# Binary cross-entropy on one core: compute pieces pipelined across chunk borders with the negation two pieces behind, and the first predictions loaded from SyncE

## The chip, the cores and the metric

The kernel runs on one core of one Trainium2 chip. The metric is device time in microseconds (us); lower is better. Executions of one kernel agree within 0.2% here. DVE is VectorE, ACT is ScalarE, POOL is GpSimd, SP is SyncE; HBM is the chip's main memory, and a DMA queue is the list of transfers that one engine has issued.

## The reference

```python
# pred, target: float32, 8192 x 8192; pred in [0.01, 0.99], target is 0 or 1
pred = np.clip(pred, 1e-7, 1 - 1e-7)
return -(target * np.log(pred) + (1 - target) * np.log(1 - pred))
```

As target is 0 or 1, this is -ln(|target - 1 + pred|), which the kernel computes.

## The kernel before

The 67.1 million elements are 524,288 columns of 128 partitions, cut into chunks of 4096, 4096, 8192, then 30 of 16384, then 8192, 4096, 2048, 1024, 1024. Two rings of 32768 columns hold predictions (float32, overwritten with the result) and targets (cast to bf16 by the load). A ring holds two big chunks, so chunk k+2 can be loaded only after chunk k was stored.

```python
RING = 32768
SUB = 2048
...
    def load(k):
        c, w = at(k), widths[k]            # at(k) = start column % RING
        nc.gpsimd.dma_start(out=ring_t[:, c : c + w], in_=dram(target_f, cols[k], w))
        nc.gpsimd.dma_start(out=ring_p[:, c : c + w], in_=dram(pred_f, cols[k], w))

    def store(k):
        c, w = at(k), widths[k]
        nc.gpsimd.dma_start(out=dram(out_f, cols[k], w), in_=ring_p[:, c : c + w])

    def front(c, w):
        ...                                # DVE: clip; DVE: p = (t - 1) + p; ACT: Abs; ACT: Ln
    def back(c, w):
        ...                                # DVE: p = p * -1

    def compute(k):
        c, w = at(k), widths[k]
        n = max(1, w // SUB)
        s = w // n
        for i in range(n):
            front(c + i * s, s)
            if i:
                back(c + (i - 1) * s, s)
        back(c + (n - 1) * s, s)           # all negations of chunk k before chunk k+1

    with tc.manual_schedule():             # every engine runs its instructions in program order
        stored = loaded = 0
        for k in range(len(widths)):
            ...                            # store what must go, load what then fits
            compute(k)
        ...                                # store the rest
```

Below, t(k), p(k) and "store k" are the target load, prediction load and store of chunk k.

Of the kernel before, what the change touches and what calls it, by code (L numbers as in the profile page):

```python
# [1 line left out]

# [4 lines left out]

EPS = 1e-7



RING = 32768

SUB = 2048


def chunk_widths(total):
    head = [4096, 4096, 8192]
    tail = [8192, 4096, 2048, 1024, 1024]
    big = 16384  # L20
    n = (total - sum(head) - sum(tail)) // big
    widths = head + [big] * n + tail
    assert sum(widths) == total
    return widths


@with_exitstack
def kernel(
    ctx: ExitStack,
    tc: tile.TileContext,  # L30
    pred: bass.AP,
    target: bass.AP,
    out: bass.AP,
):






    nc = tc.nc
    fp32 = mybir.dt.float32
    bf16 = mybir.dt.bfloat16
    Alu = mybir.AluOpType
    Act = mybir.ActivationFunctionType
    P = nc.NUM_PARTITIONS

    R, C = pred.shape
    pred_f = pred.rearrange("r c -> (r c)")
    target_f = target.rearrange("r c -> (r c)")  # L50
    out_f = out.rearrange("r c -> (r c)")
    total = R * C // P

    def dram(flat, col, w):
        return flat[col * P : (col + w) * P].rearrange("(p w) -> p w", p=P)

    pool = ctx.enter_context(tc.tile_pool(name="rings", bufs=1))
    ring_p = pool.tile([P, RING], fp32, name="ring_p", tag="ring_p")
    ring_t = pool.tile([P, RING], bf16, name="ring_t", tag="ring_t")
    warm = pool.tile([1, 8], fp32, name="warm", tag="warm")  # L60
    nc.vector.memset(warm, 1.0)  # L61
    nc.scalar.activation(out=warm, in_=warm, func=Act.Ln)  # L62

    widths = chunk_widths(total)
    cols = [sum(widths[:k]) for k in range(len(widths))]

    def at(k):
        c = cols[k] % RING
        assert c + widths[k] <= RING
        return c  # L70

    def load(k):
        c, w = at(k), widths[k]
        nc.gpsimd.dma_start(out=ring_t[:, c : c + w], in_=dram(target_f, cols[k], w))  # L74
        nc.gpsimd.dma_start(out=ring_p[:, c : c + w], in_=dram(pred_f, cols[k], w))  # L75

    def store(k):
        c, w = at(k), widths[k]
        nc.gpsimd.dma_start(out=dram(out_f, cols[k], w), in_=ring_p[:, c : c + w])  # L79

    def front(c, w):
        p, t = ring_p[:, c : c + w], ring_t[:, c : c + w]
        nc.vector.tensor_scalar(  # L83
            out=p, in0=p, scalar1=EPS, scalar2=1 - EPS, op0=Alu.max, op1=Alu.min
        )
        nc.vector.scalar_tensor_tensor(  # L86
            out=p, in0=t, scalar=1.0, in1=p, op0=Alu.subtract, op1=Alu.add
        )
        nc.scalar.activation(out=p, in_=p, func=Act.Abs)  # L89
        nc.scalar.activation(out=p, in_=p, func=Act.Ln)  # L90

    def back(c, w):
        p = ring_p[:, c : c + w]
        nc.vector.tensor_scalar(  # L94
            out=p, in0=p, scalar1=-1.0, scalar2=None, op0=Alu.mult
        )

    def compute(k):
        c, w = at(k), widths[k]
        n = max(1, w // SUB)  # L100
        s = w // n
        for i in range(n):
            front(c + i * s, s)
            if i:
                back(c + (i - 1) * s, s)
        back(c + (n - 1) * s, s)



    with tc.manual_schedule():  # L110
        stored = loaded = 0
        for k in range(len(widths)):
            while loaded < len(widths):
                end = cols[loaded] + widths[loaded]
                while stored < k and end > cols[stored] + RING:
                    store(stored)
                    stored += 1
                if end > cols[stored] + RING:
                    break
                load(loaded)  # L120
                loaded += 1
            compute(k)
        while stored < len(widths):
            store(stored)
            stored += 1


# [1 line left out]
_INS = ['pred', 'target']  # L129
_OUTS = [((8192, 8192), 'float32')]  # L130


# [23 lines left out]
```

## Time and profile before

| | before |
|---|---|
| device time | 1870.75 us median (1870.64 to 1871.0, 3 runs) |
| DVE busy, ACT busy | 1178.6 us (63%), 976.3 us (52%) |
| software DMA queue, share of 16 engines | 99.9% |
| HBM traffic | 805.3 MB, 431 GB/s over the span |
| cycle of one big chunk | 58.1 us, of which store, target and prediction about 19.4 us each |

The page of the kernel before: the span; the busy tenths of the DMA engines in 40 slices; the DMA queue; the HBM traffic.

```profile
span 1868.8 us, 1563 instructions
...
DMA  9999999999999999999999999999999999999998
...
q0 software_dynamic: 16416, 671.10, 99.9%
...
HBM read 536.87 MB, written 268.44 MB: 431 GB/s over the span
```

The DMA engines are the bound. In the trace a packet of 65,536 bytes takes 2.418 us, so 16 engines carry 16 x 65,536 / 2.418 us = 433.7 GB/s. The Trainium skill ("DMA: Bandwidth & Descriptors", section "Where 436 GB/s comes from") puts the ceiling of the 16 ports at 435.2 GB/s, with which these packets agree; that it lets HBM bind such transfers at about 358 GB/s does not hold here, where one core moved 431 GB/s, and the measurement decides. (A packet of a target load takes 2.43 us too: it reads 65,536 bytes of float32 but writes only 32,768 of bf16, so here the cast saved no time on the DMA engines.) The engines are busy from the first packet, 2.64 us after the span's start, to the last, 1.45 us before its end.

Why do they never run dry? The timeline of the kernel before around the end of one chunk (start, duration, engine, line, operation; in brackets the idle time before it and what ended it):

```profile
530.47 1.23 DVE L94 TENSOR_SCALAR ring_p<-ring_p 128x2048 f32<-128x2048 f32 x1 [2.78 <-ACT ring_p L90]
532.00 0.54 POOL L79 DMA_DIRECT2D out_dram<-ring_p  x1 [20.43 <-DVE ring_p L94]
532.52 0.55 POOL L74 DMA_DIRECT2D ring_t<-in_target_dram  x1
549.52 1.23 DVE L83 TENSOR_SCALAR ring_p<-ring_p 128x2048 f32<-128x2048 f32 x1 [17.82 <-DMA ring_p<-in_pred_dram]
```

The last negation of a chunk (L94) ends at 531.7. POOL issues its store at 532.00 and the target load two chunks on at 532.52. The next prediction load lands only at 549.5, when DVE starts its clip (L83). So at the landing 17.5 us have passed since more work was queued, and DVE's idle time there costs nothing.

The waits of the kernel before (engine and line, what it waited for: us in total, times, longest):

```profile
POOL ring_p L75 <- DMA out_dram<-ring_p: 1084.9, 30, 37.1
...
POOL out_dram L79 <- DVE ring_p L94: 689.9, 36, 25.7
DVE ring_p L83 <- DMA ring_p<-in_pred_dram: 552.9, 32, 18.8
DVE ring_p L94 <- ACT ring_p L90: 120.8, 73, 3.9
```

DVE's 120.8 us of waits for ACT are what the change is after: mainly at the end of each chunk, DVE waits for ACT with nothing else to do.

### The profile page before, as it was taken

The numbers are of one execution on the slowest core, as the hardware profiler recorded it, in microseconds if no ns is written. First come the engines' busy times: TensorE is split into PE (matmuls) and PEld (weight loads), VectorE is DVE, ScalarE is ACT, GpSimd is POOL, SyncE is SP. The second block draws the span as 40 slices with busy tenths as digits, with TensorE's granted clock in tenths as the row PEclk, the third lists the DMA queues.
The fourth block names the chain that finished last, engine by engine and source line by source line (L and its number), as shares of the span: only waits on it lengthen the run. The fifth ranks groups of instructions, "written<-read, shape, count | busy, mean of one in ns | idle before, by whom it ended". The sixth has DMA issues, their size and how long they took to land.

```text
span 1868.8 us, 1563 instructions
## 1 busy us (share of the span) xinstructions
DVE 1178.6 (63%) x772; ACT 976.3 (52%) x516; POOL 65.4 (3%) x118
## 2 busy tenths in 40 slices
DVE  4557755577555775557755577555776556755595
ACT  3446544565444654446544466444664446644474
POOL 1000000000000000000000000000000000000010
DMA  9999999999999999999999999999999999999998
GB/s 292 359 358 338 348 400 371 337 355 342 393 386 339 341 352 387 384 351 339 345 386 389 351 344 337 383 395 344 352 344 365 400 358 339 354 355 395 374 335 349
DMA packets 16427, 671.19 MB, mean 359 GB/s; under 512 B 1824, under 2 KB 1824, under 8 KB 2720
## 3 DMA queue, kind: packets, MB, share of 16 engines
q0 software_dynamic: 16416, 671.10, 99.9%
q14 instruction: 11, 0.09, 0.0%
HBM read 536.87 MB, written 268.44 MB: 431 GB/s over the span
## 4 chain that ended last, share of the span: by engine, by line
DMA 34%; issue 30%; DVE 27%; ACT 7%; POOL 1%; another core or an unknown queue 1%; POOLq 0%; PEldq 0%
DMA ring_p<-in_pred_dram 32%; DVE ring_p L86 13%; DVE ring_p L94 7%; DVE ring_p L83 7%; ACT ring_p L89 3%; ACT ring_p L90 3%; DMA out_dram<-ring_p 2%; POOL out_dram L79 1%; POOL ring_t L74 1%; POOL ring_p L75 0%; POOLq L151 0%; POOLq L79 0%; PEldq L151 0%
## 5 line engine op out<-in xcount | busy, mean ns | idle before, releaser
L89 ACT ACTIVATE ring_p<-ring_p 128x2048 f32<-128x2048 f32 (+1 forms) x257 | 488.9, 1902 | 876.0 <-DVE ring_p L86 876.0
L83 DVE TENSOR_SCALAR ring_p<-ring_p 128x2048 f32<-128x2048 f32 (+1 forms) x257 | 312.9, 1218 | 552.9 <-DMA ring_p<-in_pred_dram 552.9
L86 DVE SCALAR_TENSOR_TENSOR ring_p<-ring_t,ring_p 128x2048 f32<-128x2048 bf16 (+1 forms) x257 | 586.9, 2284 | 8.8
L90 ACT ACTIVATE ring_p<-ring_p 128x2048 f32<-128x2048 f32 (+1 forms) x257 | 489.2, 1903 | 8.1
L94 DVE TENSOR_SCALAR ring_p<-ring_p 128x2048 f32<-128x2048 f32 (+1 forms) x257 | 313.1, 1218 | 120.8 <-ACT ring_p L90 120.8
L75 POOL DMA_DIRECT2D ring_p<-in_pred_dram x38 | 21.9, 576 | 1094.1 <-DMA out_dram<-ring_p 1084.9
L79 POOL DMA_DIRECT2D out_dram<-ring_p x38 | 22.1, 581 | 700.3 <-DVE ring_p L94 689.9
L74 POOL DMA_DIRECT2D ring_t<-in_target_dram x38 | 21.8, 574 | 5.3 <-DMA ring_t<-in_target_dram 4.4
L62 ACT ACT_TABLE_LOAD x1 | 1.3, 1283 | 0.7 <-PEq L140 0.7
L61 DVE MEMSET warm<- 1x8 f32 x1 | 0.1, 65 | 0.8 <-PEq L140 0.8
L62 ACT ACTIVATE warm<-warm 1x8 f32<-1x8 f32 x1 | 0.2, 207 | 0.0
L140 POOL MEMSET const-float32-0.0<- 128x1 f32 x1 | 0.1, 98 | 0.2 <-issue 0.2
L140 POOL MEMSET const-bfloat16-1.0<- 128x1 bf16 x1 | 0.1, 101 | 0.0
L140 POOL MEMSET const-float32-1.0<- 128x1 f32 x1 | 0.1, 98 | 0.0
L140 POOL MEMSET const-uint8-127<- 128x1 uint8 x1 | 0.1, 98 | 0.0
## 6 DMA issues: line engine op xcount, KB each, us to landing
ring_t<-in_target_dram POOLq DMA_DIRECT2D x30, 4096.0 KB, 55.6
ring_p<-in_pred_dram POOLq DMA_DIRECT2D x2, 4096.0 KB, 29.1
out_dram<-ring_p POOLq DMA_DIRECT2D x2, 4096.0 KB, 30.7
ring_p<-in_pred_dram POOLq DMA_DIRECT2D x3, 2048.0 KB, 20.9
out_dram<-ring_p POOLq DMA_DIRECT2D x3, 2048.0 KB, 53.1
ring_t<-in_target_dram POOLq DMA_DIRECT2D x2, 2048.0 KB, 37.9
ring_t<-in_target_dram POOLq DMA_DIRECT2D x3, 1024.0 KB, 16.5
ring_p<-in_pred_dram POOLq DMA_DIRECT2D x1, 1024.0 KB, 30.7
```

Of the source, the lines that this page charges most:

```text
L61: nc.vector.memset(warm, 1.0)
L62: nc.scalar.activation(out=warm, in_=warm, func=Act.Ln)
L74: nc.gpsimd.dma_start(out=ring_t[:, c : c + w], in_=dram(target_f, cols[k], w))
L75: nc.gpsimd.dma_start(out=ring_p[:, c : c + w], in_=dram(pred_f, cols[k], w))
L79: nc.gpsimd.dma_start(out=dram(out_f, cols[k], w), in_=ring_p[:, c : c + w])
L83: nc.vector.tensor_scalar(out=p, in0=p, scalar1=EPS, scalar2=1 - EPS, op0=Alu.max, op1=Alu.min)
L86: nc.vector.scalar_tensor_tensor(out=p, in0=t, scalar=1.0, in1=p, op0=Alu.subtract, op1=Alu.add)
L89: nc.scalar.activation(out=p, in_=p, func=Act.Abs)
L90: nc.scalar.activation(out=p, in_=p, func=Act.Ln)
L94: nc.vector.tensor_scalar(out=p, in0=p, scalar1=-1.0, scalar2=None, op0=Alu.mult)
L140: nc = _bacc.Bacc("TRN2", target_bir_lowering=False, num_devices=1)
```

## The change

The intent: treat all pieces of all chunks as one stream, keep the negation two pieces behind the clip, so that DVE need not wait for ACT; and load the first predictions from SyncE, beside GpSimd's first target load. The diff, cut to its core:

```diff
+LAG = 2
...
-    def load(k):
+    def load_t(k):
...
+    def load_p(k):
+        c, w = at(k), widths[k]
+        queue = nc.sync if k == 0 else nc.gpsimd
+        queue.dma_start(out=ring_p[:, c : c + w], in_=dram(pred_f, cols[k], w))
...
+    pieces = []
+    for k, w in enumerate(widths):
         n = max(1, w // SUB)
         for i in range(n):
+            pieces.append((k, at(k) + i * (w // n), w // n, i == n - 1))
...
+    def load_what_fits():
+        nonlocal loaded
+        while (
+            loaded < len(widths)
+            and cols[loaded] + widths[loaded] <= (cols + [total])[stored] + RING
+        ):
+            load_t(loaded)
+            load_p(loaded)
+            loaded += 1

     with tc.manual_schedule():
...
+        load_what_fits()
+        nc.vector.memset(warm, 1.0)          # moved here from the top
+        nc.scalar.activation(out=warm, in_=warm, func=Act.Ln)
+        for i in range(len(pieces) + LAG):
+            if i < len(pieces):
+                _, c, w, _ = pieces[i]
+                front(c, w)
+            if i >= LAG:
+                k, c, w, last = pieces[i - LAG]
+                back(c, w)
+                if last:
+                    store(k)
+                    stored = k + 1
+                    load_what_fits()
```

More of the change, by code (lines that the diff above doesn't have):

```diff
@@ L60 @@
     warm = pool.tile([1, 8], fp32, name="warm", tag="warm")
-    nc.vector.memset(warm, 1.0)
-    nc.scalar.activation(out=warm, in_=warm, func=Act.Ln)
     widths = chunk_widths(total)
@@ L70, in at @@
         return c
-    def load(k):
+    def load_t(k):
         c, w = at(k), widths[k]
         nc.gpsimd.dma_start(out=ring_t[:, c : c + w], in_=dram(target_f, cols[k], w))
-        nc.gpsimd.dma_start(out=ring_p[:, c : c + w], in_=dram(pred_f, cols[k], w))
+    def load_p(k):
+        c, w = at(k), widths[k]
+        queue = nc.sync if k == 0 else nc.gpsimd
+        queue.dma_start(out=ring_p[:, c : c + w], in_=dram(pred_f, cols[k], w))
     def store(k):
@@ L96, in back @@
         )
-    def compute(k):
-        c, w = at(k), widths[k]
+    pieces = []
+    for k, w in enumerate(widths):
         n = max(1, w // SUB)
-        s = w // n
         for i in range(n):
-            front(c + i * s, s)
-            if i:
-                back(c + (i - 1) * s, s)
-        back(c + (n - 1) * s, s)
-    with tc.manual_schedule():
-        stored = loaded = 0
-        for k in range(len(widths)):
-            while loaded < len(widths):
-                end = cols[loaded] + widths[loaded]
-                while stored < k and end > cols[stored] + RING:
-                    store(stored)
-                    stored += 1
-                if end > cols[stored] + RING:
-                    break
-                load(loaded)
-                loaded += 1
-            compute(k)
-        while stored < len(widths):
-            store(stored)
-            stored += 1
+            pieces.append((k, at(k) + i * (w // n), w // n, i == n - 1))
+    stored = 0
+    loaded = 0
+    def load_what_fits():
[7 more added lines that the diff above has]
+            loaded += 1
+    with tc.manual_schedule():
+        load_what_fits()
[12 more added lines that the diff above has]
+                    load_what_fits()
 _INS = ['pred', 'target']
```

## The prediction

> **What bounds the kernel now.** The DMA engines. The page shows 9 tenths or more in nearly every slice and the software queue at 99.9% of 16 engines' time; 805.3 MB of HBM traffic at 431 GB/s over 1868.8 us. A 65,536-byte packet takes 2.418 us, so 16 engines carry 433.7 GB/s. The Trainium skill ("DMA: Bandwidth & Descriptors", Where 436 GB/s comes from) puts the ceiling at 435.2; the trace agrees. DVE (63%) and ACT (52%) wait: the waits view gives DVE 553 us on prediction loads. Only 2.7 us before the first packet and 1.5 us after the last could be saved.
>
> **Why DMA never idles.** The ring holds two 16384-column chunks, so chunk k+2 loads only after store k. In the timeline p(k+1) lands 58 us after p(k). Compute of chunk k takes 40 us; then GpSimd issues store k and t(k+2), 17.5 us before p(k+1) lands. So work is always queued. Cycle 58.1 us, pure DMA: store, target and prediction about 19.4 us each.
>
> **What the change does.** Same bytes, same instruction counts. The first prediction load on SyncE: the skill's same page (Issuing engines are not separate DMA queues) says it interleaves on the same 16 engines; at most 0.5 us either way. The lag of two pieces hides DVE waits for ACT (121 us in all, the waits view), off the critical path.
> But the lag crosses chunk borders: the last two negations of chunk k stand on DVE, in order, behind the first two clips of chunk k+1, which wait for p(k+1). Store k, and behind it on GpSimd t(k+2) and p(k+2), cannot be issued before p(k+1) has landed, and p(k+1) is the last thing in the DMA queue. The 17.5 us of queued work becomes a bubble.
>
> **Cost of one bubble**, from timeline start-to-start times:
> - DVE: clip 1.26, subtract 2.21, negate 1.14, clip 1.26, subtract 2.21, negate 1.22 = 9.3 us after the landing.
> - DVE end to GpSimd issue: 0.29 us.
> - Issue to first packet, slow first packets, landing latency: the first load pair took 3.2 us more than its bytes need, the last store 1.7 us more; estimate 2.4 us.
> Together 12.0 us; the cycle goes from 58.1 to 70.1 us.
>
> **How often.** Stores 3 to 31: 29 full bubbles, 348 us. At store 2 the queued stores 0 and 1 (9.7 us) cover most of it: 2 to 3 us. In the tail all loads are queued behind store 31, so later stores have backlog: about 0, or a few us less, because the DMA engine that lags 5 us behind the mean at the end resynchronizes each cycle.
>
> **Prediction.** 1870.75 + 348 + 2.5, less a few us: about 2217 us, 18% slower. Range 2180 to 2250 (bubble 10.8 to 13). Chances: faster by over 2%: 0.02; within 2%: 0.05; slower by over 2%: 0.93.
>
> **What would show each step.**
> - DMA share near 0 in a window of some 11 us per cycle; HBM traffic near 365 GB/s.
> - Prediction loads issued every 70 us instead of 58.
> - Stores issued 9.6 us after each prediction landing; the wait of p(k+2) for the store falls from 36 to about 21 us.
> - DVE's wait for prediction loads rises from 553 to about 900 us; its wait for ACT falls from 121 to near 0.
> - Busy times of DVE and ACT unchanged.
>
> **What would make it wrong.** If negations are scheduled ahead of the waiting clips, or stores wait on less than the last negation, there is no bubble and the time is 1868 to 1872. If an idle DMA queue restarts slower than estimated (descriptor writing slowed while DVE runs beside it), each us costs 29 us.

## The result, and the profile after

The kernel after takes 2242.69 us median (2242.44 to 2243.1, 4 runs), the kernel before 1870.88 us (1870.64 to 1871.72, 4 runs): a ratio of 1.1987, 95% interval 1.1966 to 1.2007. A ratio is the mean time of one kernel's runs over that of the other's of the same rounds, so it isn't quite the ratio of the medians.

| | before | after |
|---|---|---|
| device time, us | 1870.9 | 2242.7 |
| DVE busy, ACT busy, us | 1178.6, 976.3 | 1172.4, 979.9 |
| DMA engines wholly idle for over 3 us | never | 29 times, 334.4 us in all |
| cycle of one big chunk, us | 58.1 | 70.8 |

The same lines of the page, kernel after:

```profile
span 2241.0 us, 1564 instructions
...
DMA  9977977789778887779877797777977789778888
...
q0 software_dynamic: 16272, 669.00, 84.3%
q1 hardware_dynamic: 144, 2.10, 0.3%
...
HBM read 536.87 MB, written 268.44 MB: 359 GB/s over the span
```

The bytes are the same, the compute is the same, and the DMA engines now stand still for 15% of the span. The single load on SyncE shows as its own queue, to which the page gives 0.3% of the time of the 16 engines. The waits, kernel after:

```profile
POOL out_dram L84 <- DVE ring_p L99: 1477.2, 36, 47.0
...
DVE ring_p L88 <- DMA ring_p<-in_pred_dram: 1033.0, 34, 34.1
POOL ring_p L80 <- DMA out_dram<-ring_p: 617.4, 29, 21.4
...
DVE ring_p L99 <- ACT ring_p L95: 0.5, 1, 0.5
```

DVE's wait for ACT is gone (120.8 to 0.5 us): the change did what it was meant to. But the stores' wait for the negation has grown from 690 to 1477 us, and DVE's wait for prediction loads from 553 to 1033 us. The timeline of the kernel after at one chunk border shows why:

```profile
638.55 1.23 DVE L88 TENSOR_SCALAR ring_p<-ring_p 128x2048 f32<-128x2048 f32 x1 [33.89 <-DMA ring_p<-in_pred_dram]
639.81 2.29 DVE L91 SCALAR_TENSOR_TENSOR ring_p<-ring_t,ring_p 128x2048 f32<-128x2048 bf16 x1
642.02 1.22 DVE L99 TENSOR_SCALAR ring_p<-ring_p 128x2048 f32<-128x2048 f32 x1
...
643.15 1.22 DVE L88 TENSOR_SCALAR ring_p<-ring_p 128x2048 f32<-128x2048 f32 x1
...
644.41 2.29 DVE L91 SCALAR_TENSOR_TENSOR ring_p<-ring_t,ring_p 128x2048 f32<-128x2048 bf16 x1
646.62 1.22 DVE L99 TENSOR_SCALAR ring_p<-ring_p 128x2048 f32<-128x2048 f32 x1
...
648.13 0.96 POOL L84 DMA_DIRECT2D out_dram<-ring_p  x1 [46.82 <-DVE ring_p L99]
...
649.08 0.54 POOL L75 DMA_DIRECT2D ring_t<-in_target_dram  x1
```

The two negations (L99) at 642.02 and 646.62 belong to the old chunk, and ACT had been done with both for over 30 us. They stand in DVE's program order behind the first and the second clip (L88) of the new chunk, and the first clip waits for the new chunk's prediction load, which lands at 638.5. Only 9.6 us later is the store issued, and behind it the next target load. Meanwhile the DMA queue is empty, because that prediction load was the last thing in it. Busy time by stretch of the same border (us of the stretch, DVE, ACT and POOL busy, clock, DMA share, GB/s):

```profile
636.00:638.00 2.00, 0.00 (x0) 0.00 (x0) 0.00 (x0) 1.00 0.00 0
638.00:648.00 10.00, 9.38 (x7) 5.09 (x3) 0.00 (x0) 1.00 0.00 0
648.00:650.00 2.00, 1.97 (x2) 1.97 (x2) 1.49 (x2) 1.00 1.26 524
```

This view counts a packet in the stretch where it starts, so the share can pass 1, and the last packets before a gap stand one stretch earlier. By the packets themselves each gap is 11.53 us: 0.40 us from the last packet's end to the landing, 9.6 us on DVE and to the issue, 1.52 us from the issue's start to the first packet.

The whole difference can be added up, since the span is the first packet's start, plus the packets' time on 16 engines, plus their idle time, plus what follows the last packet. Of 372.3 us between the two profiled spans, 341.6 is idle time between the first and last packet (summed over the 16 engines it is 5428 us, against -37 before, where packets overlap a little; the difference is divided by 16), 27.3 is packets that took longer, 4.3 is a later end after the last packet, and -0.9 is an earlier first packet (1.73 against 2.64 us).

The packets that took longer are nearly all of one kind: the last packet of each engine's share of a store, 2.85 to 3.5 us instead of 2.42, some 464 of them (16 in each of 29 cycles), with the next target load right behind them. There the 16 engines start this packet within 0.1 us of one another (at 666.7 us); in the kernel before they pass from store to target spread over 2.3 us (at 567 us), and only 17 packets of this size in the whole run take over 2.8 us. So the slow packets go with engines that pass from a store to a load in step; why, no run here shows.

### The profile page after: what moved, and what is told of

Same layout as the page of the kernel before. It is cut to its first block, busy times and chain, and to the rows that moved or that the text cites. A ratio compares the mean times of both kernels' runs of the same rounds, so it can differ in the third digit from the quotient of the medians.

```text
span 2241.0 us, 1564 instructions
## 1 busy us (share of the span) xinstructions
DVE 1172.4 (52%) x772; ACT 979.9 (44%) x516; POOL 96.0 (4%) x117
## 4 chain that ended last, share of the span: by engine, by line
DMA 54%; issue 28%; DVE 14%; POOL 2%; another core or an unknown queue 1%; POOLq 0%; DVEq 0%; PEldq 0%
DMA ring_p<-in_pred_dram 52%; DVE ring_p L91 7%; DVE ring_p L88 4%; DVE ring_p L99 3%; DMA out_dram<-ring_p 2%; POOL out_dram L84 1%; POOL ring_t L75 1%; POOLq L164 0%; POOL ring_p L80 0%; POOLq L84 0%; DVEq L88 0%; PEldq L164 0%
## 5 line engine op out<-in xcount | busy, mean ns | idle before, releaser
L88 DVE TENSOR_SCALAR ring_p<-ring_p 128x2048 f32<-128x2048 f32 (+1 forms) x257 | 313.0, 1218 | 1033.0 <-DMA ring_p<-in_pred_dram 1033.0
L99 DVE TENSOR_SCALAR ring_p<-ring_p 128x2048 f32<-128x2048 f32 (+1 forms) x257 | 312.4, 1216 | 0.5 <-ACT ring_p L95 0.5
L84 POOL DMA_DIRECT2D out_dram<-ring_p x38 | 34.8, 917 | 1477.5 <-DVE ring_p L99 1477.2
L80 POOL DMA_DIRECT2D ring_p<-in_pred_dram x37 | 40.1, 1083 | 638.5 <-DMA out_dram<-ring_p 617.4
```

Source lines behind the costliest of these rows:

```text
L80: queue.dma_start(out=ring_p[:, c : c + w], in_=dram(pred_f, cols[k], w))
L88: nc.vector.tensor_scalar(out=p, in0=p, scalar1=EPS, scalar2=1 - EPS, op0=Alu.max, op1=Alu.min)
L99: nc.vector.tensor_scalar(out=p, in0=p, scalar1=-1.0, scalar2=None, op0=Alu.mult)
```

## The experiments

The theory: the lag crosses the chunk border, so store k waits for p(k+1), and nothing is queued behind p(k+1). Rivals: the second queue disturbs the software queue; crossing a border costs a fixed amount; the lag itself, or DVE running beside descriptor writing, is slow.

### e1_flush: no lag across the border

```diff
-        for i in range(len(pieces) + LAG):
-            ...
+        pending = []
+        for k, c, w, last in pieces:
+            front(c, w)
+            pending.append((c, w))
+            while pending and (last or len(pending) > LAG):
+                back(*pending.pop(0))
+            if last:
+                store(k)
+                stored = k + 1
+                load_what_fits()
```

> The kernel after, but the negations still pending are done before the first clip of the next chunk (lag of two inside a chunk, none across its border). Border theory (store k waits behind the next chunk's prediction load): no bubble, 1866 to 1873 us, predictions issued every 58 us. Rivals: if the SyncE load, the new place of the loads in the program, or the lag of two inside a chunk costs the time, it stays near 2243 us.

Measured: 1873.53 us (ratio to before 1.0013, interval 0.9998 to 1.0028), half a microsecond above the forecast; the late end, seen below in all kernels with 113 transfers on GpSimd's queue, is more than that. All but some 3 of the 372 us are gone, though the SyncE load, the place of the loads in the program and the lag of two inside a chunk all stayed. The timeline of its POOL engine shows the store again 38.7 us before the prediction load that needs its space, and cycles of 58.0 us:

```profile
646.07 0.54 POOL L84 DMA_DIRECT2D out_dram<-ring_p  x1 [17.99 <-DVE ring_p L99]
646.60 0.55 POOL L75 DMA_DIRECT2D ring_t<-in_target_dram  x1
684.76 1.36 POOL L80 DMA_DIRECT2D ring_p<-in_pred_dram  x1 [37.62 <-DMA out_dram<-ring_p]
704.10 0.54 POOL L84 DMA_DIRECT2D out_dram<-ring_p  x1 [17.99 <-DVE ring_p L99]
```

### e2_lag1 and e3_lag3: the lag in other sizes

```diff
-LAG = 2
+LAG = 1        # e2_lag1;   LAG = 3 in e3_lag3
```

> The kernel after with LAG = 1. Border theory: one clip, one subtract and one negate less after the landing of each prediction load (4.61 us), so the cycle falls from 70.8 to 66.2 us and the time to 2243 - 29 x 4.61 = 2109 us (2100 to 2118); idle gap of the DMA engines 6.9 instead of 11.5 us. A rival in which any crossing of the border costs a fixed restart predicts 2243 us; one in which DVE work elsewhere counts predicts no such step.

> The kernel after with LAG = 3. Border theory: 4.60 us more per cycle, 2243 + 30 x 4.6 = 2381 us (2370 to 2390), gap 16.1 us. A fixed cost of crossing the border: 2243 us.

Measured: 2105.7 us and 2379.95 us, within 4 us of both forecasts. The gaps of the DMA engines are 6.93 and 16.13 us, against 11.53 with a lag of two: 4.60 us for each piece of lag, which is one clip, one subtract and one negate. Stores of e2_lag1, 66.2 us apart:

```profile
607.98 0.96 POOL L84 DMA_DIRECT2D out_dram<-ring_p  x1 [42.20 <-DVE ring_p L99]
...
674.17 0.96 POOL L84 DMA_DIRECT2D out_dram<-ring_p  x1 [42.23 <-DVE ring_p L99]
```

Stores of e3_lag3, 75.4 us apart:

```profile
614.05 0.96 POOL L84 DMA_DIRECT2D out_dram<-ring_p  x1 [52.06 <-DVE ring_p L99]
...
689.43 0.96 POOL L84 DMA_DIRECT2D out_dram<-ring_p  x1 [52.09 <-DVE ring_p L99]
```

So the cost is not a fixed price of crossing the border. It is the DVE work between the landing and the last negation, plus a restart.

### e4_no_sync and e5_sync_only: the SyncE load

```diff
-        queue = nc.sync if k == 0 else nc.gpsimd
+        queue = nc.gpsimd                       # e4_no_sync: the kernel after without the SyncE load
```

e5_sync_only is the kernel before with only the line `queue = nc.sync if k == 0 else nc.gpsimd` put into its prediction load.

> The kernel after with the first prediction load back on GpSimd's queue. Border theory: 2243 us, at most 1 us more (the first packet starts 0.9 us later, at 2.64 instead of 1.73 us). Rival: if the second queue disturbs the software queue, clearly below 2243 us, down to 1870 us if it is the whole cause.

> The kernel before with only the first prediction load moved to SyncE. Border theory: 1870.9 us less 0 to 1 us, since the first packet starts about 0.9 us earlier and every byte after it is bound by the DMA engines. Rival (the second queue costs time): above 1875 us.

Measured: e4_no_sync 2238.8 us, 3.9 us faster than the kernel after; e5_sync_only 1874.64 us, 3.9 us slower than the kernel before (ratio 1.002, interval 1.0008 to 1.0033). So the load on SyncE explains 4 of the 372 us and none of the gaps, which are still 29 of 11.53 us in e4_no_sync. Both forecasts for it missed: it should have gained up to 1 us, and the kernels with it are 4 us slower. At the start it does gain: the first packet comes at 1.78 us instead of 2.64. At the end the last packet of e5_sync_only is even earlier (1866.6 against 1867.3 us), yet the span ends 6.2 us after it instead of 1.45. The trace shows that GpSimd's long DRAIN, the instruction beside its last store issue, ends 5.2 us after the last landing, against 0.37 us in the kernel before, while the other engines wait for it. In the view of SyncE's waits that is the second line. Kernel before:

```profile
SPq L151 <- DMA out_dram<-ring_p: 1866.9, 3, 1846.2
SPq L151 <- PEq L151: 0.8, 2, 0.4
```

e5_sync_only:

```profile
SPq L152 <- DMA out_dram<-ring_p: 1865.7, 5, 1856.0
SPq L152 <- PEq L152: 5.7, 2, 5.3
```

The view names PE's sequencer (PEq), which came last by its rules; the times of the DRAIN show that all were waiting for GpSimd.

### e6_small_after and e7_small_before: chunks of 8192 columns

```diff
-    big = 16384
+    big = 8192          # in the kernel after (e6) and in the kernel before (e7)
```

> The kernel after with big chunks of 8192 instead of 16384 columns, so the ring holds four and p(k+1) is not the last thing in the DMA queue: two more chunks stand behind it. Lag of two across the border kept. Border theory (what costs is that nothing is queued behind p(k+1)): 1866 to 1880 us. Rival (the lag across the border slows DVE or the engines by itself, once per border): there are twice as many borders, so 2240 us or more, up to 2600.

> The kernel before with big chunks of 8192 columns, the control for the run above: 1866 to 1880 us; if the smaller transfers cost by themselves, both show it alike.

Measured: 1878.43 us and 1878.84 us. With four chunks in the ring the full lag of two across the border, at twice as many borders, costs nothing against its control. In the waits of e6_small_after only 5 of 68 stores still wait for DVE. The line of its waits:

```profile
POOL out_dram L84 <- DVE ring_p L99: 54.8, 5, 18.8
```

In its timeline each store is issued directly after a prediction load that waited for space:

```profile
909.53 0.61 POOL L80 DMA_DIRECT2D ring_p<-in_pred_dram  x1 [27.39 <-DMA out_dram<-ring_p]
910.13 0.54 POOL L84 DMA_DIRECT2D out_dram<-ring_p  x1
910.66 0.55 POOL L75 DMA_DIRECT2D ring_t<-in_target_dram  x1
```

This is the cleanest evidence that the harm is in the emptiness of the queue and not in the order on DVE. Both end late as well (4.0 us after the last landing), although e7 has nothing on SyncE; that doesn't fit with SyncE as the cause of the late end. The rest of their 8 us against 16384 columns was not taken apart.

### e8_target_early: something else in the queue

```diff
                 front(c, w)
+                if last:
+                    load_targets(k + 1)   # t(k+2): its ring space is free once chunk k's fronts are done
```

Here the lag of two across the border stays, and `load_what_fits` leaves out a target that was already loaded this way.

> The kernel after, lag of two across the border kept, but t(k+2) is issued as soon as the fronts of chunk k are done, ahead of store k, so that 19.4 us of target load run while DVE works on the new chunk. Border theory: the 11.5 us gap is filled; a new small gap of about 2 us stays where p(k+2) waits for store k with nothing queued: cycle about 60.8 us, 1940 to 1965 us. Rival (delay of DVE or of the stores themselves costs): 2243 us.

Measured: 2001.0 us, so 242 us of the 372 are back, but 36 to 61 us fewer than I expected. The 11.5 us gap is filled; the foreseen small gap behind the store is there, 1.86 us in nearly all of 31 cycles, around 995 in these stretches:

```profile
985.00:993.00 8.00, 7.50 (x5) 6.48 (x4) 0.00 (x0) 1.00 1.19 516
993.00:996.00 3.00, 0.00 (x0) 2.25 (x2) 0.13 (x1) 1.00 0.00 0
996.00:998.00 2.00, 0.00 (x0) 0.00 (x0) 0.94 (x2) 1.00 1.50 524
```

What I had not counted is slower packets: in nearly every cycle the first packet of each engine after the gap takes about 3.1 us instead of 2.42, and the last packet of each engine's share of the target load, with the store right behind it, takes 3.0 to 4.2 us instead of 2.43 (448 packets; they make 34 us of the 54 below). The store's own last packets, with nothing behind them, are not slower (2.42 us). The packets' time on 16 engines is 1920.8 us against 1867.0 in the kernel before: 54 us, nearly as much as the 73 us of idle time.

### e9_sub4096: pieces of 4096 columns

```diff
-SUB = 2048
+SUB = 4096          # in the kernel before
```

> The kernel before with compute pieces of 4096 instead of 2048 columns, to see whether anything is left to win. Half the DVE and ACT instructions; each 8192-byte instruction-fetch packet (11 in the span) is thought to delay one DMA engine, which ends 5 us behind the mean. If so the fetches fall to some 6, the lag halves, and the time is 1867 to 1870 us. Rival (the lag has another cause): 1870 to 1872 us.

Measured: 1875.7 us, slower than the 1870.47 us of the kernel before in the same rounds (ratio 1.0026, interval 1.0014 to 1.0039). My expectation failed. The fetches did fall from 11 to 6, and the spread between the first and the last engine landing late in the run fell from 6.3 to 4.8 us, less than by half. But the tail lost more: a piece of 4096 takes longer through DVE and ACT, the last stores are issued later, and the DMA engines idle twice there, 7.8 us in all. So fetches may be part of the lag; these runs don't settle it.

### e10_tiny_sync, e13_tiny_gpsimd and e14_flush_split: the late end

Up to here the late end was seen with 113 transfers on GpSimd's queue (all kernels with the first load on SyncE) and with 203 and 204 (e6, e7), not with 114 (before, e4, e9).

```diff
+    tiny = pool.tile([1, 8], fp32, name="tiny", tag="tiny")
+    nc.sync.dma_start(out=tiny, in_=pred_f[0:8]...)      # e10: before, plus 32 bytes from SyncE
+    nc.gpsimd.dma_start(out=tiny, in_=pred_f[0:8]...)    # e13: the same from GpSimd instead
```

e14_flush_split is e1_flush with the target load of chunk 3 issued as two halves, so that GpSimd's queue has 114 transfers beside the 2 MB load on SyncE.

> The kernel before plus one 32-byte load from SyncE at the start; the 114 transfers of GpSimd's queue stay. The runs with the SyncE load end 5 us after the last DMA packet instead of 1.45 us. If any use of SyncE's queue costs that at the end: about 1875 us (1873.5 to 1876), GpSimd's last drain ends over 4 us after the last landing. If it is the number of transfers on GpSimd's queue (113 there, 114 in the kernel before): 1871 us.

> The kernel before plus the same 32-byte load, but from GpSimd's queue, so it has 115 transfers and SyncE none. If the late end belongs to SyncE's queue: 1871 to 1872 us. If it hangs on the number of transfers of GpSimd's queue (203, 204 and 113 ended late, 114 ended promptly): about 1875 us.

> The kernel with the lag flushed at the chunk border and the first load on SyncE (1873.5 us), with one target load (of chunk 3) issued as two halves, so that GpSimd's queue has 114 transfers again, as in the kernel before. Its profile ended 5.4 us after the last landing. The late end was seen with 113, 203 and 204 transfers on that queue and not with 114 or 115, whatever SyncE did. If the count on GpSimd's queue sets it: the drain ends 0.4 us after the last landing and the time is 1869.2 us (1868.5 to 1870), below the kernel before. If a 2 MB load on SyncE's queue is what makes it late (a 32-byte one did not): 1873.5 us, 4.7 us after the last landing.

Measured: e10_tiny_sync 1870.51 us and e13_tiny_gpsimd 1871.43 us, both ending 0.37 us after the last landing; e14_flush_split 1868.86 us, also 0.37 us. Its line of SyncE's waits:

```profile
SPq L171 <- PEq L171: 0.8, 2, 0.4
```

e14 keeps the 2 MB load on SyncE, adds one transfer on GpSimd's queue, and the 4.7 us of e1_flush are gone. So use of SyncE's queue is neither enough to make the end late (e14) nor needed for it (e7); it goes with what is queued on GpSimd. Over the 14 kernels profiled, 113, 203 and 204 transfers end 4.0 to 5.2 us late, 114 and 115 don't. Which property of the queue it is (a count, a position in a descriptor ring) stays open.

e14_flush_split also answers whether the change has a good part: its ratio to the kernel before is 0.9987, interval 0.9974 to 1.0001, so a gain of 0.1%, at most 0.3%, and not clear of noise. It keeps the SyncE load (first packet at 1.77 instead of 2.64 us) and drops the lag across the border. No kernel here beats the one before clearly; at 99.9% of the DMA engines' time there is nearly nothing left.

## Why the prediction was right

It said 2217 us, range 2180 to 2250; measured 2242.7, only 7 us below the upper end. Point by point:

- **The mechanism** (two negations of chunk k behind clips that wait for p(k+1), store and loads behind them, an empty DMA queue) is shown by e1_flush, which removes the crossing and the 372 us with it; by e2 and e3, which scale it; and by e6 and e8, which keep the crossing and give the queue something to do.
- **How often**: 29 full gaps forecast, 29 found.
- **The DVE part and issue** of a gap: 9.6 us forecast, 9.6 measured (landing 638.5, issue 648.13).
- **The waits**: p(k+2) for the store from 36 to 21 us forecast, 21.3 measured; DVE for ACT near 0 forecast, 0.5 measured. DVE's wait for predictions was forecast at 900 and is 1033 us: the 121 us it no longer waits for ACT it now waits there, which I had left out.
- **The restart was sized too small.** I put "Issue to first packet, slow first packets, landing latency" at 2.4 us. In the cycle measured, from the issue of the store to the landing of the next prediction load is 709.29 - 648.13 = 61.16 us, against the 58.1 us that the bytes take: 3.1 us. Over 29 cycles the 0.7 us make about 19 of the 26 us that the forecast is low. The parts: 1.52 us from issue to first packet, 0.40 landing, and about 0.94 from slower packets (27.3 us over 29), chiefly the last ones of each store, which I had not foreseen; the remaining 0.2 was not taken apart. The rest of the 26 us is the late end less the earlier start (3.4 us) and the "few us less" below.
- **SyncE**: "at most 0.5 us either way" was wrong. e4_no_sync shows 3.9 us between with and without it, and the trace puts 4.3 at the end, minus 0.9 at the start. The cause is not SyncE (e10, e14), but with that transfer taken off GpSimd's queue the late end came, and with e14's added one it went.
- The "few us less" that I took off for the lagging engine did not show up as a gain.

On the restart the Trainium skill is close: "DMA: Bandwidth & Descriptors", section "Anatomy of one DMA", gives a fixed cost of about 2.0 us per DMA on GpSimd's path; here issue to first packet plus landing is 1.52 + 0.40 = 1.92 us. With work always queued (the kernel before, 114 transfers, DMA engines 99.9% busy) it is hidden. In this restart POOL's issue takes 0.96 us, with a DVE clip running beside it, instead of 0.54 with DVE idle, and the first packet comes 1.52 us after the issue's start instead of 1.10 (the last store of the kernel before). The skill describes GpSimd locked out of descriptor writing while DVE runs an operation in a 2-port mode ("SBUF — State Buffer", section "SBUF: two separate sides"). The kept traces fit with that and narrow it: in all 14 together, after the first 10 us, and by what DVE does in an issue's first 0.5 us, an issue on POOL takes 0.54 us (median) with DVE idle (556 issues) and no more beside the subtract alone (628), both never over 0.6, but 0.96 us beside a clip or negation alone (374, up to 2.0). That the clip and negation run in such a mode is not shown.

## What to carry to other kernels

Before deepening a software pipeline across the border of a buffer, ask what the delayed step releases: here a negation of 1.2 us released the store, and the store released the loads, so delaying it behind an instruction that waits for the next load closed a loop and left the DMA queue empty once per chunk. Waits on an engine with slack (120 us of DVE here) are not worth removing when the price is the order in which buffers come free. If such a lag is wanted, give the DMA queue something that doesn't depend on it (smaller chunks in the same ring), and then check that it gains anything.

## What the Trainium skill lacked or had wrong

- None of the pages looked at has the late end: GpSimd's long DRAIN ends 4.0 to 5.2 us after the last landing with 113, 203 or 204 transfers on its queue, and 0.37 us with 114 or 115. It belongs to "DMA: Bandwidth & Descriptors" beside the fixed costs.
- The same page gives the fixed cost per DMA as about 2.0 us, most of it the write receipt. Here, of 1.92 us, 1.52 stand before the first packet and 0.40 after the last. With DVE idle it was 1.10 before and 0.35 after, for the last store of the kernel before. With the slower packets that follow (2.85 to 3.5 us instead of 2.42 at the end of each store), a restart of a drained queue cost 3.1 us.
- The page states first-byte latencies of about 1 us for GpSimd's path and 0.6 us for SyncE's (Specifications). From the start of the issue to the first packet at the span's start these runs show 1.37 us (1.27 to 2.64) and 0.99 us (0.74 to 1.73): the difference agrees, the sizes are 0.4 us larger.
- The same page's section "Where 436 GB/s comes from" has HBM bind transfers between HBM and the core at about 358 GB/s. Here one core moved 431 GB/s over the whole span.
